# Modulation tiles in two buffers of their own, loaded from GpSimd's queue, and partly summed during the second V projection

## The chip, the cores and the metric

The kernel runs on one core of one Trainium2 chip. The metric is the device time of one execution in microseconds (us). A core has TensorE (PE, with its weight load PEld), VectorE (DVE), ScalarE (ACT), GpSimd (POOL) and SyncE (SP), each with an in-order instruction queue of its own. Loads are issued here from SyncE's queue, stores also from ScalarE's and GpSimd's.

## The reference

One layer of a backbone: x is (1, 512, 2048), the context (1, 256, 2048), all in float32.

```python
mx = silu(c) @ w_mod + b_mod                    # 2048 -> 6 x 2048: sh1, sc1, gt1, sh2, sc2, gt2
hc = modulate(rmsnorm(ctx, norm1_g), sh1c, sc1c)  # the same with c_ctx, for the context
hx = modulate(rmsnorm(x, norm1_g), sh1, sc1)
q, k, v, g, lf, lb, cb, cc, cx = split_proj(hx @ w_in)   # context: the same weights
o_x = gla_bidir(q, k, v, gates(lf), gates(lb), states of the context)  # 4 heads, chunks
mix = concat(rmsnorm(o_x) * gla_g * silu(g), cb * conv_grid(cc * cx, conv_w)) @ w_out
x = x + gt1 * mix
h2 = modulate(rmsnorm(x, norm2_g), sh2, sc2)
x = x + gt2 * (silu(h2 @ w_gate) * (h2 @ w_up)) @ w_down
return rmsnorm(x, final_g)
```

What matters here is the first line: the four later parts of the modulation, gt1, sh2, sc2 and gt2 (8192 numbers, each a product of silu(c) with 2048 weights), are not needed before the output projection.

## The kernel before

**Products.** Every large product runs on TensorE as three matmuls (`mm3`), of a high and a low part of both operands. A weight tile of 128 x 1024 is loaded into a buffer called `raw` (`load_raw`), cast on ScalarE to `whi` (line 102) and subtracted on VectorE to `wlo` (line 103); `whi` and `wlo` have three buffers each. A weight split in this text is line 103.

**Modulation tiles.** The 64 tiles of `wm2` hold the transposed weights of the four later parts: 128 outputs by 2048 inputs each. `mod_some(n, last)` adds n to what is owed and, for each whole tile owed, loads two halves of 128 x 1024 (512 KB each) into `raw` buffers. For each half VectorE multiplies by the broadcast silu(c) (`cbc`) and sums along the row (line 382, in the profile CUSTOM_DVE_ANT_0, followed by a short reading of the accumulator into `modacc`). These 128 are the sums of this text.

**Stages.** (1) scale and K projection; (2) first V projection (`wv[0]`), in which chunks of hx and hc are shifted as soon as they are used (`shift_chunk`, whose first step is an addition on GpSimd, and whose result also goes to the low-rank gate product, `lf_part`, `pl` in the profile); (3) second V projection (`wv[1]`, 16 steps of 18 matmuls, a weight tile for two steps), with the last four chunks shifted in its first four steps and then `shares`: sixteen more loads into `raw`, which TensorE multiplies directly (`pb`) to get the bias of K and V; (4) the weave: context states, gates, then four heads. In it `weave` takes turns between a stage of attention and a weight tile's worth of projection (`fill`), and calls `mod_some(MOD_STEP, 64)` after each, so that the modulation tiles are spread over the weave; (5) output projection and the feed-forward network.

**Order.** Up to the end of the weave a scheduler orders the instructions of every engine when the program is built: it takes what its own estimates say is ready first, with the order of the code as priority. So a load or a sum may stand well ahead of the place where the code has it. From the output projection on, SyncE's order is the code's. All raw loads, weights and modulation halves, go through SyncE's queue and take the next of four `raw` buffers; a load whose buffer is not free holds up all loads behind it.

Of the kernel before, what the change touches and what calls it, by code (L numbers as in the profile page):

```python
# [7 lines left out]
F32 = mybir.dt.float32  # L8
# [5 lines left out]
P = 128  # L14
# [39 lines left out]
def tile_hybrid_block(  # L54
# [6 lines left out]
    nc = tc.nc  # L61
# [3 lines left out]
    wpool = ctx.enter_context(tc.tile_pool(name="wpool", bufs=1))  # L65
# [14 lines left out]
    def bank(name="bank"):  # L80
        return pspool.tile([P, 512], F32, tag="g", name=name, bufs=5)

    def abank(name="abank"):
        return pspool.tile([P, 512], F32, tag="a", name=name, bufs=3)

    def banks6():
        return [abank("acc6") for _ in range(3)] + [bank("acc6") for _ in range(3)]

    def mm(o, l, r, start, stop):
        nc.tensor.matmul(o, l, r, start=start, stop=stop, skip_group_check=True)  # L90

    def mm3(o, l, r, start, stop):

        mm(o, l[1], r[0], start, False)
        mm(o, l[0], r[1], False, False)
        mm(o, l[0], r[0], False, stop)

    def sl(pair, *idx):
        return pair[0][idx], pair[1][idx]
# [12 lines left out]
        nc.scalar.activation(hi, src, AF.Identity, bias=shift)  # L112
        nc.vector.scalar_tensor_tensor(lo, src, shift, hi.bitcast(F32), op0=ALU.add, op1=ALU.subtract)

    def load_raw(src):
        n = src.shape[-1]
        r = wpool.tile([P, 1024], F32, tag="raw", name="raw", bufs=4)
        nc.sync.dma_start(r[:, :n], src)
        return r[:, :n]

    def load_w(src, k, eng=None):

        r = load_raw(src)
        n = r.shape[-1]
        hi = wpool.tile([P, 1024], F32R, tag="whi", name="whi", bufs=3)
        lo = wpool.tile([P, 1024], F32R, tag="wlo", name="wlo", bufs=3)
        split(hi[:, :n], lo[:, :n], r, eng)
        return (hi[:, :n].rearrange("p (k n) -> p k n", k=k),
                lo[:, :n].rearrange("p (k n) -> p k n", k=k))
# [179 lines left out]
    def shift_chunk(i):  # L309

        for n, h, rb, q in ((SEQ, hx[i], rbx, 0), (CTX, hc[i], rbc, 1)):
            t = hcpool.tile([P, n], F32, tag=f"sq{q}", name="ht", bufs=2)
            nc.gpsimd.tensor_tensor(t, h[0].bitcast(F32), h[1].bitcast(F32), op=ALU.add)
            nc.vector.tensor_tensor(t, t, rb, op=ALU.mult)
            sh = shs[:, i, q : q + 1]
            if q == 0:
                nc.vector.tensor_scalar(t, t, sh, None, op0=ALU.add)
                split(h[0], h[1], t)
                hraw[i] = t
            else:  # L320
                split_shifted(h[0], h[1], t, sh)

    def stat(i, tt):
        if tt < NX:
            return sl(hx[i], ALL, slice(tt * P, tt * P + P))
        return sl(hc[i], ALL, slice((tt - NX) * P, (tt - NX) * P + P))

    def lf_part(pl, i):
        j = 32 * (i % 4)
        mm(pl[j : j + 32, :], wl3[:, i, :], hraw[i], i < 4, i >= 12)  # L330

    def lf_finish(pl, a, n):

        t = hcpool.tile([P, SEQ], F32, tag="lfs", name="lfs", bufs=1)
        nc.scalar.copy(t[:, :n], pl[:, :n])
        ps = bank("ps")
        mm(ps[:32, :n], smt[:, S_QUAD : S_QUAD + 32], t[:, :n], True, True)
        nc.scalar.copy(lfT[:32, a : a + n], ps[:32, :n])
# [36 lines left out]
    def mod_some(n, last):  # L375

        owed[0] += n
        while owed[0] >= 1 and nmod[0] < last:
            j = nmod[0]
            for hf in range(2):  # L380
                w = load_raw(wm2[j][:, hf * 1024 : hf * 1024 + 1024])
                nc.vector.tensor_tensor_reduce(  # L382
                    out=w, in0=w, in1=cbc[:, hf * 1024 : hf * 1024 + 1024], scale=1.0, scalar=0.0,
                    op0=ALU.mult, op1=ALU.add, accum_out=modacc[:, j, hf : hf + 1])
            nmod[0] += 1
            owed[0] -= 1

    MOD_STEP = 0.85

    def mod_finish(a, b):  # L390
        nc.vector.tensor_tensor(modv[:, a:b], modacc[:, a:b, 0], modacc[:, a:b, 1], op=ALU.add)
        nc.vector.tensor_tensor(modv[:, a:b], modv[:, a:b], colt[:, C_BMOD + 32 + a : C_BMOD + 32 + b], op=ALU.add)


    def shares(i):
# [6 lines left out]
        if i % 8 == 0:  # L402
            sh_t["pb"] = bank("pb")
        pb = sh_t["pb"]
        w = load_raw((wk if i < 8 else wv[0])[i % 8]).rearrange("p (k n) -> p k n", k=2)
        for kk in range(2):
            k = 2 * (i % 8) + kk
            jj = 32 * (k % 4)
            mm(pb[jj : jj + 32, :], shs[:, k, :], w[:, kk, :], k < 4, k >= 12)
        if i % 8 == 7:  # L410
# [15 lines left out]
            else:  # L426
# [4 lines left out]
                for hh in range(2):  # L431
                    for t2 in range(2):
                        for u in range(2):
                            v = vx[hh][t2][:, u, :]
                            nc.vector.tensor_tensor(v, v, pbx[:, hh * DV : hh * DV + DV], op=ALU.add)
    sh_t = {}
    accv = banks6()
    for i in range(KD):
        if i % 2 == 0:
            wvp = load_w(wv[1, i // 2], 2)  # L440
        for tt in range(NX + NCT):
            mm3(accv[tt], stat(i, tt), sl(wvp, ALL, i % 2), i == 0, i == KD - 1)
        if i < 4:
            shift_chunk(KD - 4 + i)
        if i < 5:
            lf_part(pl, KD - 5 + i)
        elif i == 5:
            lf_finish(pl, 0, SEQ)
        else:
            for k in ((2 * i - 12, 2 * i - 11) if i < 12 else (i,)):  # L450
                shares(k)
# [83 lines left out]
    def weave(stages, fill):  # L535

        for _ in stages:
            next(fill, None)
            mod_some(MOD_STEP, 64)
        for _ in fill:  # L540
            mod_some(MOD_STEP, 64)

# [132 lines left out]
    for h in range(HEADS):  # L675
# [3 lines left out]
        if h + 2 < HEADS:  # L679
            fill.insert(0, do_q(h + 2))  # L680
        weave(do_gla(h), (None for g in fill for _ in g))
    mod_some(64, 64)
    mod_finish(0, 64)
    nc.vector.tensor_scalar(gsc2, modv[:, 32:48], 1.0, None, op0=ALU.add)
    nc.vector.tensor_tensor(gsc2, gsc2, colt[:, C_G2 : C_G2 + KD], op=ALU.mult)
# [256 lines left out]
    for p in range(NBD // 2):  # L942
# [20 lines left out]
        w = lambda b, u: wo[p, b, u]  # L963
# [280 lines left out]
```

## Time and profile before

| | us |
|---|---|
| median of 3 runs (2349.32 to 2352.01) | 2351.49 |
| the profiled execution | 2355.56 |
| its span, first to last instruction | 2353.8 |
| TensorE busy | 2270.1 |
| VectorE busy | 1671.7 |
| the 128 sums, busy | 156.4 |
| VectorE idle just ahead of the sums | 199.0 |
| first and last issue of a modulation load, from the span's start | 302.6, 831.2 |

The profile gives for a group of instructions how often it ran, the busy time, the mean of one, and the idle time of the engine just before it with what ended that idle time. `out<-in` are the program's names of tiles. In a timeline a row has start, duration, engine, line and, in brackets, the idle time before it. In a list of waits a row has who waited for whom, the sum in us, how often, and the longest.

### The profile page before, as it was taken

The numbers are of one execution on the slowest core, as the hardware profiler recorded it, in microseconds if no ns is written. First come the engines' busy times: TensorE is split into PE (matmuls) and PEld (weight loads), VectorE is DVE, ScalarE is ACT, GpSimd is POOL, SyncE is SP. The second block draws the span as 40 slices with busy tenths as digits, with TensorE's granted clock in tenths as the row PEclk, the third lists the DMA queues.
The fourth block names the chain that finished last, engine by engine and source line by source line (L and its number), as shares of the span: only waits on it lengthen the run. The fifth ranks groups of instructions, "written<-read, shape, count | busy, mean of one in ns | idle before, by whom it ended". The sixth has DMA issues, their size and how long they took to land.

```text
span 2353.8 us, 27801 instructions
## 1 busy us (share of the span) xinstructions
PE 2270.1 (96%) x10328; PEld 1807.0 (77%) x10328; DVE 1671.7 (71%) x2066; ACT 1002.5 (43%) x1349; POOL 136.1 (6%) x186
## 2 busy tenths in 40 slices
PE   8999999999989899999999999999999999999996
PEld 4765667787777778787888888888888878888875
DVE  3566164665555757779888788878887877787888
ACT  3433055233232324465544554455445544443343
POOL 2423000000000000000000000000000000000001
PEclk9999999999999999999999999999999999999998
DMA  9773365666656654544434643464345585756634
GB/s 329 225 258 121 134 223 171 202 195 193 196 188 189 205 183 147 179 155 126 160 117 152 205 144 120 149 206 144 125 143 206 191 316 178 274 176 198 243 128 137
DMA packets 161619, 431.43 MB, mean 183 GB/s; under 512 B 17867, under 2 KB 38635, under 8 KB 161356
## 3 DMA queue, kind: packets, MB, share of 16 engines
q1 hardware_dynamic: 141612, 380.87, 49.2%
q0 software_dynamic: 8720, 28.58, 3.2%
q10 hardware_dynamic: 11152, 20.21, 2.3%
q8 instruction: 81, 1.33, 0.2%
q14 instruction: 54, 0.44, 0.1%
HBM read 380.82 MB, written 48.78 MB: 183 GB/s over the span
## 4 chain that ended last, share of the span: by engine, by line
PE 50%; DVE 5%; DMA 2%; issue 1%; ACT 1%; SPq 0%; POOL 0%; DVEq 0%; POOLq 0%; ACTq 0%
PE acc L90 49%; DVE wlo L103 2%; DMA raw<-wd 1%; PE pt L990 1%; DMA raw<-wu 1%; PE pt L90 1%; DVE y L1102 0%; DVE y L1122 0%; ACT whi L102 0%; DVE ch L818 0%; DVE y L1114 0%; DMA ch<-wd 0%; DVE y L1113 0%; DVE ch L799 0%; DVE hbig L959 0%
## 5 line engine op out<-in xcount | busy, mean ns | idle before, releaser
L102 ACT CAST whi<-ch 128x1024 fp32r<-128x1024 f32 x350 | 368.7, 1054 | 433.4 <-PE acc L90 361.2
L103 DVE TENSOR_TENSOR wlo<-ch,whi 128x1024 fp32r<-128x1024 f32 x350 | 425.9, 1221 | 139.2 <-ACT whi L102 138.1
L102 ACT CAST whi<-raw 128x1024 fp32r<-128x1024 f32 x252 | 264.4, 1051 | 438.8 <-PE acc L90 250.5
L103 DVE TENSOR_TENSOR wlo<-raw,whi 128x1024 fp32r<-128x1024 f32 x252 | 312.0, 1239 | 168.4 <-ACT whi L102 167.8
L382 DVE CUSTOM_DVE_ANT_0 raw<-raw,cbc 128x1024 f32<-128x1024 f32 x128 | 156.4, 1224 | 199.0 <-DMA raw<-wm 196.1
L90 PE MATMUL acc<-hhl,whi 128*128 128x512 f32 x640 | 201.2, 395 | 0.0
L90 PE MATMUL acc<-hhi,wlo 128*128 128x512 f32 x320 | 135.5, 425 | 17.8 <-DVE wlo L103 17.1
L90 PEld LDWEIGHTS acc<-hhl,whi 128*128 128x128 f32 x640 | 122.2, 191 | 28.2 <-issue 2.5
L90 PE MATMUL acc<-hhl,wlo 128*128 128x512 f32 x320 | 128.4, 401 | 0.0
L90 PE MATMUL acc<-hlo,whi 128*128 128x512 f32 x320 | 127.5, 399 | 0.2 <-DVE hlo L108 0.2
L90 PE MATMUL acc<-hhi,whi 128*128 128x512 f32 x320 | 127.6, 399 | 0.0
L90 PE MATMUL acc<-whi,a6l 128*128 128x512 f32 x312 | 122.7, 394 | 4.0 <-DVE big L838 2.6
L90 PE MATMUL acc<-wlo,a0h 128*128 128x512 f32 x312 | 123.3, 395 | 2.1 <-DVE wlo L103 2.1
L90 PE MATMUL acc<-wlo,a6h 128*128 128x512 f32 x312 | 122.7, 393 | 0.9 <-DVE wlo L103 0.9
L90 PE MATMUL acc<-whi,a6h 128*128 128x512 f32 x312 | 122.6, 393 | 0.0
L90 PE MATMUL acc<-wlo,a5h 128*128 128x512 f32 x312 | 121.7, 390 | 0.9 <-DVE wlo L103 0.9
L90 PE MATMUL acc<-whi,a0h 128*128 128x512 f32 x312 | 122.3, 392 | 0.0
L90 PE MATMUL acc<-whi,a0l 128*128 128x512 f32 x312 | 121.8, 391 | 0.0
L90 PE MATMUL acc<-whi,a5l 128*128 128x512 f32 x312 | 121.5, 389 | 0.0
L90 PE MATMUL acc<-whi,a5h 128*128 128x512 f32 x312 | 121.5, 389 | 0.0
L90 PE MATMUL acc<-whi,a2l 128*128 128x512 f32 x280 | 109.7, 394 | 4.8 <-ACT whi L102 4.8
L90 PE MATMUL acc<-wlo,a1h 128*128 128x512 f32 x280 | 109.2, 390 | 1.5 <-DVE wlo L103 1.5
(301 smaller groups left out, 4761.6 us busy)
## 6 DMA issues: line engine op xcount, KB each, us to landing
raw<-wm SPq DMA_DIRECT2D x128, 512.0 KB, 4.7
raw<-wu SPq DMA_DIRECT2D x92, 512.0 KB, 4.4
ch<-wu SPq DMA_DIRECT2D x88, 512.0 KB, 3.8
raw<-wc SPq DMA_DIRECT2D x48, 512.0 KB, 4.0
raw<-wd SPq DMA_DIRECT2D x47, 512.0 KB, 6.6
ch<-wd SPq DMA_DIRECT2D x44, 512.0 KB, 5.9
opd<-oh ACTq DMA_DIRECT2D x77, 256.0 KB, 3.0
opd<-ol POOLq DMA_DIRECT2D x77, 256.0 KB, 3.5
```

The lines of the kernel that those rows point to most:

```text
L90: nc.tensor.matmul(o, l, r, start=start, stop=stop, skip_group_check=True)
L102: nc.scalar.copy(hi, src)
L103: (eng or nc.vector).tensor_tensor(lo, src, hi, op=ALU.subtract)
L382: nc.vector.tensor_tensor_reduce(out=w, in0=w, in1=cbc[:, hf * 1024 : hf * 1024 + 1024], scale=1.0, scalar=0.0, op0=ALU.mult, op1=ALU.add, ...
L990: nc.tensor.transpose(pt[:, (2 * i + t) * P : (2 * i + t) * P + P], acts[j][2 * hf + t][:, q * P : q * P + P], ident)
```

## The change

`load_raw` gets a flag `mod`. A modulation half goes into a buffer of the tag `raw2` (two buffers) and its load is issued from GpSimd. While `mod_room` is set, from the second V projection to the end of the weave, all other raw loads use the tag `raw` (two buffers); outside of it they alternate between the two tags. `mod_some(1, 64)` is called in each of the 16 steps of the second V projection, and MOD_STEP falls from 0.85 to 0.65.

```diff
+    nraw, mod_room = [0], [False]
+
+    def load_raw(src, mod=False):
+
         n = src.shape[-1]
-        r = wpool.tile([P, 1024], F32, tag="raw", name="raw", bufs=4)
-        nc.sync.dma_start(r[:, :n], src)
+        nraw[0] += 1
+        second = mod if mod or mod_room[0] else nraw[0] % 2
+        r = wpool.tile([P, 1024], F32, tag="raw2" if second else "raw", name="raw", bufs=2)
+        (nc.gpsimd if mod else nc.sync).dma_start(r[:, :n], src)
         return r[:, :n]
...
-                w = load_raw(wm2[j][:, hf * 1024 : hf * 1024 + 1024])
+                w = load_raw(wm2[j][:, hf * 1024 : hf * 1024 + 1024], True)
...
-    MOD_STEP = 0.85
+    MOD_STEP = 0.65
...
     sh_t = {}
+    mod_room[0] = True
     accv = banks6()
     for i in range(KD):
...
             mm3(accv[tt], stat(i, tt), sl(wvp, ALL, i % 2), i == 0, i == KD - 1)
+        mod_some(1, 64)
...
     mod_some(64, 64)
+    mod_room[0] = False
     mod_finish(0, 64)
```

The scheduler moves the sums further than the code does. On VectorE, before, the late part of the second V projection reads as follows (the accumulator readings behind each sum are left out, here and below; `acc6_1874` is an accumulator of that projection, copied at its end, `raw_` with `cbc` is a sum):

```order
L103 TENSOR_TENSOR wlo_2277<-raw_2274,whi_2276 128x1024
L103 TENSOR_TENSOR wlo_2331<-raw_2328,whi_2330 128x1024
L103 TENSOR_TENSOR wlo_2436<-raw_2433,whi_2435 128x1024
L103 TENSOR_TENSOR wlo_2479<-raw_2476,whi_2478 128x1024
L382 ISA raw_2506,modacc_73<-raw_2506,cbc_76 128x1024
L382 ISA raw_2509,modacc_73<-raw_2509,cbc_76 128x1024
L459 COPY big_2410<-acc6_1874 128x512
```

There the last two weight splits of the projection and two of the next stand ahead of the first two sums of the program. Now, between the same last two weight splits:

```order
L103 TENSOR_TENSOR wlo_2349<-raw_2346,whi_2348 128x1024
L387 ISA raw_2974,modacc_73<-raw_2974,cbc_76 128x1024
L387 ISA raw_2977,modacc_73<-raw_2977,cbc_76 128x1024
L387 ISA raw_3043,modacc_73<-raw_3043,cbc_76 128x1024
L387 ISA raw_3046,modacc_73<-raw_3046,cbc_76 128x1024
L387 ISA raw_3079,modacc_73<-raw_3079,cbc_76 128x1024
L103 TENSOR_TENSOR wlo_2415<-raw_2412,whi_2414 128x1024
L387 ISA raw_3082,modacc_73<-raw_3082,cbc_76 128x1024
```

Five sums stand between two splits, each behind its own load. Counted over the whole order, 17 sums stand ahead of the first V projection's end, 53 ahead of the second's, and all 128 ahead of the middle of head 1; before, these were 0, 2 and some 60.

On GpSimd, before, at the last of the shifted chunks (`ht` is the addition that begins a chunk's shift; `hbig` with MEMSET clears a mask buffer for the heads):

```order
L313 TENSOR_TENSOR ht_1930<-hhl_890 128x512
L313 TENSOR_TENSOR ht_1966<-hhi_966,hlo_967 128x512
L313 TENSOR_TENSOR ht_1996<-hhl_1007 128x512
L552 MEMSET hbig_2659 128x512
L552 MEMSET hbig_2661 128x512
L961 DMA xnd_5897<-xn_6080 128x512
L961 DMA xnd_5897<-xn_6082 128x512
```

And now, at the same place:

```order
L318 TENSOR_TENSOR ht_1984<-hhi_966,hlo_967 128x512
L123 DMA raw_2294<-wm2 128x1024
L318 TENSOR_TENSOR ht_2020<-hhl_1007 128x512
L123 DMA raw_2328<-wm2 128x1024
L123 DMA raw_2331<-wm2 128x1024
L123 DMA raw_2370<-wm2 128x1024
L123 DMA raw_2373<-wm2 128x1024
L123 DMA raw_2400<-wm2 128x1024
L123 DMA raw_2403<-wm2 128x1024
L123 DMA raw_2436<-wm2 128x1024
L123 DMA raw_2439<-wm2 128x1024
L559 MEMSET hbig_2743 128x512
```

The modulation loads stand between the chunks' additions, and each of them waits for the sum two halves before it, and with it what is behind it on GpSimd.

More of the change, by code (lines that the diff above doesn't have):

```diff
@@ L113, in split_shifted @@
         nc.vector.scalar_tensor_tensor(lo, src, shift, hi.bitcast(F32), op0=ALU.add, op1=ALU.subtract)
-    def load_raw(src):
+    nraw, mod_room = [0], [False]
+    def load_raw(src, mod=False):
         n = src.shape[-1]
-        r = wpool.tile([P, 1024], F32, tag="raw", name="raw", bufs=4)
-        nc.sync.dma_start(r[:, :n], src)
+        nraw[0] += 1
+        second = mod if mod or mod_room[0] else nraw[0] % 2
+        r = wpool.tile([P, 1024], F32, tag="raw2" if second else "raw", name="raw", bufs=2)
+        (nc.gpsimd if mod else nc.sync).dma_start(r[:, :n], src)
         return r[:, :n]
```

## The prediction

> **What bounds the kernel now.** I read the page first (busy shares, then the groups), then who waited for whom in three stretches, then the timeline of VectorE and GpSimd where the change puts its work.
>
> ```profile
> PE 2270.1 (96%) x10328; PEld 1807.0 (77%) x10328; DVE 1671.7 (71%) x2066; ACT 1002.5 (43%) x1349; POOL 136.1 (6%) x186
> L382 DVE CUSTOM_DVE_ANT_0 raw<-raw,cbc 128x1024 f32<-128x1024 f32 x128 | 156.4, 1224 | 199.0 <-DMA raw<-wm 196.1
> ```
>
> TensorE is busy nearly throughout, so time can only come from its gaps. The second row is what the change touches: 128 half-tile sums on VectorE, 1.22 us each, before which VectorE idled 196 us waiting for their own loads. A table by stretch shows where TensorE has gaps: the second V projection (213 to 311 us), the context, the gates and head 0 (311 to 550), heads 1 to 3 (550 to 850).
>
> ```profile
> core 0: us, PE busy (x) PEld busy (x) DVE busy (x) ACT busy (x) POOL busy (x), PEclk, DMA share, GB/s
> 213.00:311.00 98.00, 97.56 (x455) 63.53 (x453) 27.40 (x40) 17.65 (x30) 8.26 (x8) 1.00 0.39 129
> 311.00:550.00 239.00, 229.31 (x995) 178.68 (x993) 144.70 (x242) 103.36 (x141) 0.00 (x0) 0.98 0.62 197
> 550.00:850.00 300.00, 276.15 (x1236) 225.63 (x1236) 184.62 (x326) 89.28 (x159) 0.00 (x0) 0.97 0.60 190
> ```
>
> The V projection has no gap worth naming, its VectorE is idle for 71 of 98 us, and its granted clock is 1.00. The middle stretch has 9.7 us of gaps, heads 1 to 3 have 23.85, and both run below full clock. Who ends TensorE's gaps in heads 1 to 3, and what VectorE itself waited for there:
>
> ```profile
> PE acc L90 <- DVE wlo L103: 8.6, 7, 2.5
> PE pd L90 <- DVE hbig L606: 5.0, 2, 4.1
> PE po L90 <- ACT sm L620: 4.3, 5, 1.5
> PE psc L90 <- DVE ke L589: 4.2, 1, 4.2
> PE psc L90 <- ACT a0h L102: 1.1, 1, 1.1
> DVE raw L382 <- DMA raw<-wm: 114.2, 48, 5.7
> ```
>
> Three of the five are VectorE being late (17.8 us), and the one thing VectorE waited for at length is the modulation tile at the head of its queue, behind which weight splits and head work stand.
>
> **The change, part by part.** No instruction is added or removed: 128 loads of 512 KB move from SyncE's queue to GpSimd's; the four raw buffers become two for weights and two for modulation halves; and the sums move forward. By the order of the built program, VectorE has 17 sums ahead of the copies that end the first V projection (0 before), 53 ahead of those that end the second (2 before), and all 128 ahead of the weight split that ran at 550.02 us (60 ahead of it and 68 behind it before), so heads 1 to 3 have nearly none left. I price the four stretches apart.
>
> **The pace of a sum.** With two buffers, each holds a half for one round trip: the sum, the handover to GpSimd, the load, the wake of VectorE. These rows price it:
>
> ```profile
> 306.34 1.23 DVE L382 CUSTOM_DVE_ANT_0 raw<-raw,cbc 128x1024 f32<-128x1024 f32 x1 [1.24 <-DMA raw<-wm]
> 1145.04 0.68 DVE L103 TENSOR_TENSOR ol<-pt,oh 128x512 fp32r<-128x512 f32 x1
> 1146.12 0.54 POOL L1004 DMA_DIRECT2D opd<-ol  x1 [2.76 <-DVE ol L103]
> DMA to landing us min/median/max: 3.5/4.7/7.2
> opd<-oh ACTq DMA_DIRECT2D x77, 256.0 KB, 3.0
> opd<-ol POOLq DMA_DIRECT2D x77, 256.0 KB, 3.5
> ```
>
> The sum takes 1.23; from the end of a VectorE operation to the GpSimd load that waited for it pass 1146.12 - 1145.72 = 0.4. The landing row is that of the 128 modulation loads. GpSimd's issue lands 0.5 later than ScalarE's of the same size (last two rows). No row shows a 512 KB load from GpSimd. Its lower bound is the fastest landing seen, 3.5; its upper bound is the median and the 0.5, 5.2. Before, up to four raw loads stood in one queue; now at most two halves do, beside one or two weights, so I take the middle, 4.35, and 0.1 for the wake. A round trip is 1.23 + 0.4 + 4.35 + 0.1 = 6.1 us, and two buffers give a sum each 3.05 us (2.6 to 3.45 at the bounds).
>
> By the Trainium skill (DMA: Bandwidth & Descriptors, the section on the anatomy of one DMA on the GpSimd path) such a load takes about 2.0 us and its bytes over 436 GB/s, which for 512 KB makes 3.2 us, a pace of 2.5 us and, by the sum below, the 2321.5 us of the second rival; the trace has no 512 KB load from GpSimd to set against it, and the quickest one from SyncE took 3.5.
>
> **First V projection: +1 us.** The 17 sums (21 us) lie in VectorE's idle time there. GpSimd's additions, with which the shift of a chunk starts, now stand behind loads that wait for a sum. The tightest chunk shows what that may cost (its shifted value, then TensorE's use of it):
>
> ```profile
> 171.32 0.48 DVE L317 TENSOR_SCALAR ht<-ht,silsh 128x512 f32<-128x512 f32 x1
> 177.79 1.04 PE L90 MATMUL pl<-ht,big 128*32 128x512 f32 x2
> ```
>
> It is ready 6 us early, which one sum and part of a load's wait fill without harm; I leave 1 us (0 to 5).
>
> **Second V projection: +18 us.** Here the cover is gone, because VectorE works in order and the splits that feed TensorE now stand behind sums:
>
> ```profile
> 234.82 0.69 DVE L103 TENSOR_TENSOR hhl<-ht,hhl 128x512 fp32r<-128x512 f32 x1 [0.74 <-ACT hhl L102]
> 258.34 1.23 DVE L103 TENSOR_TENSOR wlo<-raw,whi 128x1024 fp32r<-128x1024 f32 x1 [22.83 <-ACT whi L102]
> 294.33 1.23 DVE L103 TENSOR_TENSOR wlo<-raw,whi 128x1024 fp32r<-128x1024 f32 x1 [7.44 <-ACT whi L102]
> 311.16 1.28 DVE L459 COPY big<-acc 128x512 f32<-128x512 f32 x2
> 550.02 1.23 DVE L103 TENSOR_TENSOR wlo<-raw,whi 128x1024 fp32r<-128x1024 f32 x1 [1.18 <-ACT whi L102]
> ```
>
> The first row is the last shifted chunk. Between it and the next weight split now stand 11 sums, then 6, 5 and 5 between the later splits and 4 up to the copy of 311.16: 31 in all. The chunk ends at 235.5; the five sums put among the chunks before it delay it by 3 us, to 238.5. Two halves are already loaded (2 x 1.2), 29 come at the pace: 238.5 + 2.4 + 29 x 3.05 = 329.4, against 311.2, so +18. With pace 2.6 it is 316.3 (+5), with 3.45 it is 341 (+30). A floor comes from the other half of the edit: weights and the sixteen bias loads (pb) now share two buffers, and each is reloaded only when TensorE or the split has let go of it. Four weight tiles stand behind such loads, and four are waited for already:
>
> ```profile
> raw<-wv SPq DMA_DIRECT2D x12, 512.0 KB, 4.2
> ACT whi L102 <- DMA raw<-wv: 39.7, 4, 11.8
> ```
>
> With a landing of 4.2 us that is mostly under TensorE's work I estimate 2 us more for each of the four, so the stretch loses at least 8.
>
> **Context, gates and head 0: -3 us.** From the copy at 311.16 to the split at 550.02 are 239 us, with 58 sums before and 75 now. At the pace these are 229 us. VectorE's other work there (144.7 busy less 58 x 1.23, 73 us) mostly fits into the 3.6 us that a pair of sums leaves idle; where it stands in clusters it doesn't (the row of copies and additions after 311.16, the products of head 0), and I put 10 us for these: 239, so 0. VectorE was ahead of need there:
>
> ```profile
> 558.08 0.58 PE L90 MATMUL acc<-hhi,wlo 128*128 128x512 f32 x1
> ```
>
> TensorE took that split up 6.8 us after its end; I let half of this stock go, so -3. It cannot gain more than its gaps (9.7) and the clock (2% of 239, 4.8): -14. With pace 3.45 it is 259 + 10 - 239 - 3 = +27.
>
> **Heads 1 to 3: -25 us.** With no sum left, VectorE loses 114 us of waiting and its lateness. Gaps ended by VectorE go (17.8); the chain of ScalarE's scaled states (5.4 together) stays, since its links are not the sums. The clock row, 0.97 of 300 us, is 9 us of slower matmuls behind such gaps, of which I take 7. Bounds: -13 (only the weight splits, 8.6, and half of the clock) and -33 (23.85 + 9). The work behind the last sum (mod_finish) has 300 us more time; nothing waits for it earlier.
>
> After the weave the loads alternate between the two pairs, which is four buffers in turn as before: 0.
>
> **Sum:** +1 + 18 - 3 - 25 = -9 us. The profiled execution (span 2353.8, 2355.56 with what lies around it) would come to 2346.5; the median of the runs is 4.1 lower, 2351.5, so I forecast 2342.5. Each 0.1 us of pace moves the sum by 2.9 + 7.5 = 10.4 us, so this forecast is a balance of two large terms.
>
> **Rivals.** (1) Slower: the round trip of the modulation buffers becomes the bound of everything up to head 1. It decides from a pace of 3.14 us, a landing of 4.5. For it: the median landing now is 4.7 from a quicker queue. Against it: the halves' own queue is nearly empty. At pace 3.3 (landing 4.85) the sum is +17: 2368.5. (2) Well faster: the landing is near its minimum, 3.5 to 3.9, TensorE bounds the middle again, and the sum is +1 + 8 - 14 - 25 = -30: 2321.5 (with the largest head gain, 2313.5). (3) No change: the heads keep their gaps because ScalarE's chain, not VectorE, sets them (-15 in place of -25): +1, 2352.5. (4) The change does not do what it says: in the built order it is not 16 tiles by the second projection's end but 26; had it been 16, the V term would be at its floor of 8; the built order is what the sums above count.
>
> **Chances.** Forecast (-20 to -5 us) 0.33; rival 1 0.30; rival 2 0.20; rival 3 0.17. A change within 0.2% (4.7 us) is what a measurement here cannot tell from none. So faster 0.53, same 0.17, slower 0.30. The range runs from 2317 (most of rival 2) to 2372 (rival 1 up to pace 3.33); alone, the likeliest case has 2331 to 2347.
>
> **What would show it.** Right: VectorE's wait for the modulation load remains, now before 560 us and not after; the second V projection ends near 330; TensorE's gaps in heads 1 to 3 shrink to some 6 us and the clock there rises to 0.99 or more. GpSimd's loads land in about 4.3 us. Wrong: landings of 4.7 or more (then the split that ran at 550 comes later than 565 and the time rises), of under 3.9 (then the projection ends before 322), or gaps in heads 1 to 3 that stay with ScalarE's chain at their head.

## The result, and the profile after

The changed kernel took 2386.35 us (median; 2383.88 to 2392.41) against 2350.88 of the kernel before on the same chip: 1.0149 times as long, with a 95% interval of 1.0132 to 1.0166. It is slower by 35 us, where 9 us less had been forecast. The profiled execution took 2392.41 us, with a span of 2390.6.

The page after, TensorE and the group of the sums (count, busy time and mean of one, idle time just before them):

```profile
PE 2286.1 (96%) x10328; PEld 1814.8 (76%) x10328; DVE 1678.0 (70%) x2066; ACT 1004.1 (42%) x1349; POOL 207.3 (9%) x314
L387 DVE CUSTOM_DVE_ANT_0 raw<-raw,cbc 128x1024 f32<-128x1024 f32 x128 | 158.4, 1239 | 169.0 <-DMA raw<-wm 168.8
```

VectorE's wait for the modulation loads fell from 196 to 169 us, and the kernel still became slower. So what counts is where these waits stand. I cut both traces at the same work: the first matmul of the second V projection (214 us before, 231 after), of the weave's first weight tile (311, 366), of the tile whose split ran at 550 (558, 639) and of the last tiles of the weave (895, 935). The stretches before, in the columns of the prediction's table:

```profile
118.00:214.00 96.00, 93.99 (x444) 57.40 (x445) 58.05 (x89) 29.74 (x47) 24.77 (x22) 1.00 0.65 222
214.00:311.00 97.00, 97.00 (x452) 63.38 (x449) 27.05 (x39) 16.93 (x28) 8.26 (x8) 1.00 0.39 128
311.00:558.00 247.00, 236.20 (x1024) 184.09 (x1023) 150.14 (x250) 105.95 (x145) 0.00 (x0) 0.98 0.62 197
558.00:895.00 337.00, 312.37 (x1391) 255.73 (x1391) 196.09 (x343) 96.82 (x171) 1.23 (x2) 0.96 0.59 189
```

The same work after:

```profile
118.00:231.00 113.00, 99.34 (x446) 60.28 (x445) 76.03 (x119) 27.42 (x42) 35.85 (x40) 0.92 0.75 257
231.00:366.00 135.00, 113.81 (x452) 67.97 (x450) 71.40 (x114) 18.71 (x35) 29.49 (x45) 0.90 0.70 230
366.00:639.00 273.00, 249.11 (x1023) 192.62 (x1024) 169.35 (x282) 107.05 (x145) 38.78 (x73) 0.93 0.64 210
639.00:935.00 296.00, 296.00 (x1387) 248.37 (x1386) 120.60 (x205) 96.97 (x170) 0.84 (x2) 1.00 0.30 96
```

First V projection +17 us, second +38, context, gates and head 0 +26, the heads behind them -41: +40 in all, of which some 3 us come back behind the weave. The heads do what was hoped, and more: TensorE is busy in all 296 us, at full clock. The three stretches that took in the sums pay 81 us for it. Each pays twice: in the second V projection TensorE has 21.2 us of gaps (0 before), and its matmuls, at a clock of 0.90 in place of 1.00, take 16.8 us longer (113.81 - 97.00). In the heads both come back: 24.6 us of gaps and 16.4 of slower matmuls.

The sums of the first three stretches, one row each, and the landing of their loads:

```profile
L387 DVE CUSTOM_DVE_ANT_0 raw<-raw,cbc 128x1024 f32<-128x1024 f32 x16 | 20.4, 1274 | 25.5 <-DMA raw<-wm 25.4
L387 DVE CUSTOM_DVE_ANT_0 raw<-raw,cbc 128x1024 f32<-128x1024 f32 x37 | 46.4, 1253 | 59.7 <-DMA raw<-wm 59.7
L387 DVE CUSTOM_DVE_ANT_0 raw<-raw,cbc 128x1024 f32<-128x1024 f32 x75 | 91.7, 1224 | 83.8 <-DMA raw<-wm 83.7
raw<-wm POOLq DMA_DIRECT2D x128, 512.0 KB, 4.6
```

The second V projection holds 37 sums in 135 us, one in 3.65; the next stretch 75 in 273, one in 3.64. That the two buffers set this pace the trace shows: from the start of a sum to that of the sum two later, which takes the same buffer, pass 7.2 us on average in the first of these stretches and 6.9 in the second. Of these, 0.4 to 0.5 go to the issue of the next load, 4.9 and 4.7 to its landing, 0.6 until the sum starts and 1.2 to the sum. This is the first rival's picture.

In the first V projection the loads fall into the bursts in which SyncE loads `wsh`. One such chain, from the timelines of GpSimd, VectorE, ScalarE and TensorE:

```profile
189.62 0.57 POOL L123 DMA_DIRECT2D raw<-wm  x1 [1.50 <-DVE modacc L387]
198.00 1.23 DVE L387 CUSTOM_DVE_ANT_0 raw<-raw,cbc 128x1024 f32<-128x1024 f32 x1 [3.86 <-DMA raw<-wm]
199.15 0.48 DVE L322 TENSOR_SCALAR ht<-ht,silsh 128x512 f32<-128x512 f32 x1
199.72 0.62 ACT L102 CAST hhl<-ht 128x512 fp32r<-128x512 f32 x1 [7.22 <-DVE ht L322]
201.19 0.58 ACT L223 COPY tm<-pm 128x512 f32<-128x512 f32 x1
201.82 1.86 PE L90 MATMUL pc<-smt,tm 128*128 128x2 f32 x8 [6.62 <-ACT tm L223]
```

The load took 8.4 us to land. The sum at the head of VectorE's queue held the shift of a chunk, this held ScalarE's cast, behind which stood the copy of a shift row's product, and TensorE stood still for 6.62 us. An idle VectorE did not help: what it was to do next stood behind the sum.

That is one half of the stretch's 13.7 us of gaps. The other is TensorE waiting for `wsh` itself, whose loads in this stretch landed in 5.6 us at the median before and in 6.7 now. TensorE's wait for them, before and after:

```profile
PE pm L90 <- DMA big<-wsh: 2.0, 3, 0.8
PE pm L90 <- DMA big<-wsh: 7.0, 3, 3.4
```

### The profile page after: what moved, and what is told of

Its sections match the earlier page's. It is cut to its first block, busy times and chain, and to the rows that moved or that the text cites. A ratio compares the mean times of both kernels' runs of the same rounds, so it can differ in the third digit from the quotient of the medians.

```text
span 2390.6 us, 27833 instructions
## 1 busy us (share of the span) xinstructions
PE 2286.1 (96%) x10328; PEld 1814.8 (76%) x10328; DVE 1678.0 (70%) x2066; ACT 1004.1 (42%) x1349; POOL 207.3 (9%) x314
## 4 chain that ended last, share of the span: by engine, by line
issue 52%; PE 36%; DVE 4%; POOL 4%; DMA 3%; ACT 1%; POOLq 0%; SPq 0%; DVEq 0%; ACTq 0%
PE acc L90 32%; DMA raw<-wm 2%; POOL raw L123 2%; DVE wlo L103 2%; POOL opd L1012 1%; PE pm L90 1%; PE pt L90 1%; PE po L90 1%; DVE raw L387 0%; ACT whi L102 0%; POOL out L1131 0%; PE pd L90 0%; DMA raw<-wk 0%; PE pl L90 0%; PE pc L90 0%
## 5 line engine op out<-in xcount | busy, mean ns | idle before, releaser
L102 ACT CAST whi<-ch 128x1024 fp32r<-128x1024 f32 x350 | 368.9, 1054 | 430.9 <-PE acc L90 361.1
L102 ACT CAST whi<-raw 128x1024 fp32r<-128x1024 f32 x252 | 264.7, 1051 | 481.9 <-PE acc L90 292.3
L1012 POOL DMA_DIRECT2D opd<-ol x77 | 41.8, 543 | 880.4 <-DVE ol L103 880.4
```

What stands on the lines that cost most here:

```text
L102: nc.scalar.copy(hi, src)
L1012: nc.gpsimd.dma_start(opd[j][i, 1].rearrange("p k t -> p (k t)"), lo.bitcast(F32))
```

## Experiments: what the parts cost

All ratios are to the kernel before, run on the same chip. The line of the sums, 382 before and 387 after, is another by a few in some of these kernels.

**The queue alone** (`e1`). Edit against the kernel before:

```diff
-    def load_raw(src):
+    def load_raw(src, mod=False):
...
-        nc.sync.dma_start(r[:, :n], src)
+        (nc.gpsimd if mod else nc.sync).dma_start(r[:, :n], src)
...
-                w = load_raw(wm2[j][:, hf * 1024 : hf * 1024 + 1024])
+                w = load_raw(wm2[j][:, hf * 1024 : hf * 1024 + 1024], True)
```

> The kernel before, with the modulation loads issued from GpSimd and nothing else changed: four shared buffers, the sums where they stood before (in the built order none ahead of the first V projection's end, 0 ahead of the second's last splits, 60 ahead of the split that ran at 550 us, the same counts as in the kernel before). Theory 1 (the loss comes from the order: sums that stand ahead of the weight splits and wait there for a round trip through two buffers): V projections within 1 us of before, all of it within 10 us of before (2341 to 2361). Rival (GpSimd's queue itself is the cause, its landings are longer or disturb SyncE's loads): slower by 15 us or more, 2366 upwards, with the loss in the weave.

2376.65 us, 1.0106 (1.0083 to 1.0130), 28.6 us slower, all of it in the weave: my theory that only the order counts fell here. VectorE's wait for these loads in the weave, before and here:

```profile
DVE raw L382 <- DMA raw<-wm: 194.8, 91, 5.7
DVE raw L382 <- DMA raw<-wm: 224.3, 97, 5.4
```

It waits 29.5 us more, about as much as the kernel lost. The landing is not the reason (median 4.6 us here, 4.7 before). The handover is what differs: on SyncE a load that waited for a sum is issued 0.03 us after the end of its reading (658.78, rows further down), on GpSimd 0.4 us after VectorE lets the buffer go:

```profile
488.21 1.22 DVE L103 TENSOR_TENSOR wlo<-raw,whi 128x1024 fp32r<-128x1024 f32 x1
489.83 0.53 POOL L118 DMA_DIRECT2D raw<-wm  x1 [7.12 <-DVE wlo L103]
```

Nearly all of the 128 loads show the same two figures, 0.41 here and 0.03 before. One handover for each of the 64 tiles, at 0.4 us, would make 26 us. This is an estimate, and this run alone does not show that the handover is the whole cause. What it shows is that in the kernel before the waits in the weave were not spare: lengthening them lengthened the program.

**The buffers alone** (`e2`): the changed kernel with the loads on SyncE's queue, without the calls, MOD_STEP 0.85. The line of the queue:

```diff
-        (nc.gpsimd if mod else nc.sync).dma_start(r[:, :n], src)
+        nc.sync.dma_start(r[:, :n], src)
```

> The changed kernel with the modulation loads back on SyncE's queue, and without the calls in the second V projection: buffers of their own alone. In the built order 4 sums stand ahead of the first V projection's end, 38 ahead of the second's (changed kernel 10 and 53 by the same count, before 0 and 0). Theory 1 (the order): the loss of the V projections shrinks with the sums ahead, to some 4 us in the first and 25 in the second (changed kernel 16.5 and 39), total 2360 to 2380. Rival (GpSimd's queue is the cause): V projections within 5 us of before and a total below 2350.

2344.60 us, 0.9982 (0.9966 to 0.9999). Both expectations hold in part: the total is the rival's, but the second V projection still lost 23 us, as the order would have it, and the heads gave back 39. Queue and buffers thus are 29 and -3 us alone and 35 together.

**The calls** (`e12`): the changed kernel without `mod_some(1, 64)` in the second V projection and with the old MOD_STEP.

```diff
-    MOD_STEP = 0.65
+    MOD_STEP = 0.85
...
-        mod_some(1, 64)
```

> The changed kernel without the calls in the second V projection and with MOD_STEP 0.85 as before. The counts of sums at every place are those of the changed kernel. Theory (own buffers move the sums forward, and the calls and the step change nothing): within 5 us of the changed kernel, 2381 to 2391. Rival (the calls matter): below 2375.

2389.03 us, 1.0158 (1.0129 to 1.0187): no change. The calls in the second V projection, the last part of the change's title, do nothing. With own buffers the scheduler moves the sums forward by itself, as far as it believes the loads to be there.

**No sum before a given point** (`e3`, `e4`). The silu(c) that every sum reads is made to depend on the last copy of the first V projection (`vc[NCT - 1][0]`), or of the second (`[1]`, the lines moved behind it, without the calls and with the old MOD_STEP); the edit of `e3`:

```diff
-    nc.scalar.activation(cbc, cbc, AF.Silu)
+    late = cpool.tile([P, 1], F32, name="late")
+    nc.vector.tensor_scalar(late, vc[NCT - 1][0][:, 0:1], 0.0, 1.0, op0=ALU.mult, op1=ALU.add)
+    nc.scalar.activation(cbc, cbc, AF.Silu, scale=late)
```

> The changed kernel, with the silu(c) that the sums need made to depend on the last copy of the first V projection, so that no sum can stand ahead of its end (built order: 0 there, 37 ahead of the second projection's end, 115 ahead of the split that ran at 550). Theory 1: the 16.5 us of the first projection come back whole, the second loses by its sums, about 37/53 of 39, 27 us; the rest as in the changed kernel (mid +25, heads -40): total near 2363 (2355 to 2372). Rival (two buffers for the weights, not the sums, slow the second projection): it still loses 35 us or more, total 2370 or above.

> The same with the dependence on the last copy of the second V projection: no sum ahead of it (built order 0 there, 77 ahead of the split that ran at 550, all 128 ahead of head 2). Theory 1: both V projections within 3 us of before; the middle stretch slower by some 20 us, the heads faster by 30: total near 2342 (2333 to 2356). Rival (two buffers for the weights and the bias loads): the second projection still loses 15 us or more, although not one sum stands in it, and the total is above 2356.

2376.64 us (1.0105, 1.0077 to 1.0133) and 2376.99 us (1.0112, 1.0078 to 1.0147). With no sum in the first projection its loss is gone whole (0.0 us against before), so the sums there, with their loads, cost the 16.5 us. But then the second projection lost 43.9 us, not 27. The two in `e3`:

```profile
118.00:214.00 96.00, 93.94 (x443) 57.36 (x445) 56.81 (x89) 26.45 (x45) 25.80 (x24) 1.00 0.65 222
214.00:355.00 141.00, 112.23 (x455) 67.08 (x451) 69.71 (x114) 20.47 (x31) 27.77 (x45) 0.90 0.66 217
```

And with no sum in either, the second still lost 18: the rival's case.

**Two buffers for the weights** (`e5`): `e4`, with `mod_room` set only behind the second V projection.

```diff
-    mod_room[0] = True
     accv = banks6()
...
+    mod_room[0] = True
     lf_finish(sh_t["pl"], SEQ, CTX)
```

> The kernel of the run with no sum ahead of the second V projection's end, but now the weights and the sixteen bias loads of that projection alternate between both pairs of raw buffers (the weights are confined to one pair only after it). That run lost 18 us in the projection without a sum in it. Theory (two raw buffers for weights and bias loads cost it): the projection is back within 3 us of the kernel before, the total 15 us below that run, near 2362 (2355 to 2368). Rival (the loss came from something else, such as the loads already waiting on GpSimd): it still loses 12 us or more, total 2372 or above.

2359.00 us, 1.0035 (1.0019 to 1.0051), 18 us below `e4`. The second projection of `e4` and of `e5`:

```profile
214.00:330.00 116.00, 106.89 (x459) 66.05 (x459) 26.58 (x41) 16.54 (x29) 8.25 (x8) 0.94 0.31 101
214.00:311.00 97.00, 97.00 (x453) 63.76 (x452) 26.21 (x39) 17.11 (x29) 9.49 (x10) 1.00 0.35 121
```

So confining eight weight tiles and sixteen bias loads to two buffers costs some 18 us by itself. The versions on GpSimd's queue now make a ladder: 2359 with own buffers and the sums behind the V projections, 2377 with two buffers for the second projection's weights, 2377 with the sums in it as well (what they cost there, the heads give back), and 2386 to 2389 with sums in the first projection.

## Experiments: a head start for the loads

In the kernel before, the weave reads like this on VectorE and SyncE (timelines; the accumulator's readings and small copies are left out):

```profile
657.52 1.22 DVE L382 CUSTOM_DVE_ANT_0 raw<-raw,cbc 128x1024 f32<-128x1024 f32 x1
658.78 1.65 SPq L118 DMA_DIRECT2D raw<-wm  x2
664.85 1.23 DVE L382 CUSTOM_DVE_ANT_0 raw<-raw,cbc 128x1024 f32<-128x1024 f32 x1 [2.86 <-DMA raw<-wm]
666.12 1.23 DVE L382 CUSTOM_DVE_ANT_0 raw<-raw,cbc 128x1024 f32<-128x1024 f32 x1
667.27 1.22 DVE L103 TENSOR_TENSOR wlo<-raw,whi 128x1024 fp32r<-128x1024 f32 x1
```

The sums free the buffers, the next two loads go out, and the next sum that VectorE meets is theirs; the weight split stands behind it. The scheduler puts a sum where it expects its load, and the load comes later than that. So I tied each tile's two sums to the latest weight cast, by a write of two numbers of that cast into the place of their result:

```diff
+    cast = [None]
...
         split(hi[:, :n], lo[:, :n], r, eng)
+        cast[0] = hi
...
             j = nmod[0]
+            nc.scalar.copy(modacc[:, j, :], cast[0][:, 0:2].bitcast(F32))
             for hf in range(2):
```

It went into `e5` (GpSimd's queue, own buffers) in place of the dependence of silu(c), into the same with SyncE's queue, and into the kernel before (shared buffers, SyncE).

> As the run before, and each modulation tile's two sums are tied to the latest weight cast (ScalarE writes two numbers of that cast into the place of their result first), so that VectorE's order spreads them: 14 to 16 in eight weight tiles, 56 ahead of the split that ran at 550, in place of 17 to 22 and 78. Own buffers and GpSimd's queue stay. Theory 1 (what costs is sums standing closer together than a buffer's round trip of 6.5 us, 3.4 a sum): VectorE waits less than 40 us for these loads (169 in the changed kernel), no stretch is slower than before by over 5 us, total 2318 to 2343. Rival (GpSimd's queue costs by itself, as with shared buffers, where it lost 28 us): total 2360 or above.

> The same with the modulation loads on SyncE's queue. Theory 1: the same within 5 us (2318 to 2345), since the loads are issued a weight tile ahead of their use on either queue. Rival A (the handover of 0.4 us and the queue matter): faster than GpSimd's by 8 us or more. Rival B (a modulation load whose buffer is taken holds up the weights behind it on SyncE): slower than GpSimd's by 8 us or more.

> The kernel before (four shared buffers, SyncE's queue) with nothing but the tie of each tile's sums to the latest weight cast. Counts of sums by place within 4 of the kernel before. Theory (the even spacing alone is worth something): 2330 to 2345. Rival (what the kernel before loses is loads that stand behind other raw loads for a shared buffer, so own buffers are needed): within 5 us of before, 2343 to 2353.

2298.22 us (0.9779, 0.9745 to 0.9813), 2294.60 us (0.9776, 0.9731 to 0.9820) and 2293.70 us (0.9761, 0.9727 to 0.9795). All three beat both kernels; I had expected the first two 20 to 50 us slower, and that the shared buffers would be as good I had not expected at all: both cases of `e8` missed. The sums in the three pages:

```profile
L389 DVE CUSTOM_DVE_ANT_0 raw<-raw,cbc 128x1024 f32<-128x1024 f32 x128 | 155.3, 1222 | 105.6 <-DMA raw<-wm 100.9 <-ACT po L649 1.7 <-ACT on L648 1.4
L389 DVE CUSTOM_DVE_ANT_0 raw<-raw,cbc 128x1024 f32<-128x1024 f32 x128 | 155.1, 1222 | 58.8 <-DMA raw<-wm 55.1 <-ACT po L649 1.6 <-ACT modacc L386 1.2
L386 DVE CUSTOM_DVE_ANT_0 raw<-raw,cbc 128x1024 f32<-128x1024 f32 x128 | 152.9, 1220 | 11.9 <-DMA raw<-wm 8.7 <-issue 1.9 <-ACT modacc L383 1.2
```

In the last one VectorE hardly waits any more. The place in its trace that answers to the one above, and its weave (context to head 0, then the heads):

```profile
646.63 1.47 SPq L120 DMA_DIRECT2D raw<-wm  x2
658.51 1.23 DVE L103 TENSOR_TENSOR wlo<-raw,whi 128x1024 fp32r<-128x1024 f32 x1 [5.87 <-ACT whi L102]
659.65 1.22 DVE L386 CUSTOM_DVE_ANT_0 raw<-raw,cbc 128x1024 f32<-128x1024 f32 x1
659.76 1.47 SPq L120 DMA_DIRECT2D raw<-wm  x2
...
315.00:544.00 229.00, 229.00 (x1028) 182.30 (x1027) 148.49 (x246) 111.83 (x175) 0.00 (x0) 1.00 0.63 210
544.00:840.00 296.00, 296.00 (x1388) 248.40 (x1387) 198.55 (x345) 101.63 (x203) 0.65 (x1) 1.00 0.66 218
```

The split goes first, the sum behind it, and its load is long there (loads that were under way at 646.63 had landed by 653.5). TensorE is busy without a gap at full clock with the same 128 sums, in shared buffers and at a higher rate than before (first to last sum 475 us in place of 530). So what this pair differs by is not room, nor the number of sums per microsecond, but when a split gets its turn. The traces show it for each pair with and without the tie. From the end of a weight's cast on ScalarE to the start of its split on VectorE, the average of the weave's 80 splits is 5.8 us before and 0.3 here, 3.8 in `e5` and 1.8 in `e6`, 6.2 in `e1` and 0.4 with the tie (`e11` below).

How long VectorE waits in all is another matter. In `e6` I had expected under 40 us of waits for the loads; there are 100.9, and the kernel is only 4.5 us behind `e8`. From the end of the second projection on, `e5` and `e6`:

```profile
311.00:580.00 269.00, 241.30 (x1022) 186.23 (x1021) 173.12 (x287) 109.03 (x147) 42.31 (x80) 0.97 0.65 217
311.00:560.00 249.00, 249.00 (x1115) 198.91 (x1115) 162.53 (x273) 121.02 (x197) 34.77 (x66) 1.00 0.65 213
```

VectorE still waits 40.6 us for the loads in the second row, and TensorE has no gap: these waits hold no split for long. Most of the gain, then, is there although the loads still come late. The 4.5 us between `e6` and `e8` no run divides among loads in time, queue and buffers.

The first V projection of `e8` took 4.6 us more than before, with no sum in it. There TensorE waited 3.8 us for `wsh` in place of 2.0, and its clock was 0.97 (118 to 219 us) in place of 1.00; why, I did not follow up.

**Is it the head start, or the tie as such?** (`e9`): `e6` with the sums too close for two buffers.

```diff
-    MOD_STEP = 0.85
+    MOD_STEP = 1.3
```

> The paced kernel with GpSimd's queue and own buffers (MOD_STEP 0.85, 2298.2 us), now with MOD_STEP 1.3: 20 to 24 sums in eight weight tiles in place of 14, 85 ahead of the split that ran at 550 in place of 56, the tie kept. Eight weight tiles take TensorE some 58 us when it isn't held up, so that is a sum every 2.4 to 2.9 us, under the 3.4 us that a sum through two buffers took. Theory 1 (spacing against the round trip decides): slow again, near the unpaced kernel with the same buffers (2359), 2350 to 2385, with VectorE waiting over 130 us for the loads. Rival (the tie helps in another way, say by the priority it gives the weight splits): under 2320.

2372.45 us, 1.0089 (1.0065 to 1.0113): slow again, with the tie in place, and the splits start 4.2 us after their casts. So the tie helps only as long as the sums are not closer together than the buffers' round trip allows. VectorE's wait:

```profile
DVE raw L389 <- DMA raw<-wm: 135.8, 90, 3.5
```

**The change with the tie** (`e10`), **and the queue with the tie** (`e11`: the kernel before with GpSimd's queue, as `e1`).

> The changed kernel as it is (own buffers, GpSimd's queue, calls in the second V projection, MOD_STEP 0.65) with the tie alone added: now 0 sums ahead of the first V projection's end, 32 ahead of the second's, 76 ahead of the split that ran at 550, 122 ahead of the middle of head 2. Theory 1: the first projection as before; the second loses the 18 us that two raw buffers cost it, and up to 11 more, because 32 sums in 98 us are one in 3.06; the weave gains some 50: total 2312 to 2330. Rival (the work in the second projection is harmful by itself): 2340 or more.

> The kernel before with GpSimd's queue for the modulation loads (which alone cost 28 us) and the tie. Theory 1 (the 0.4 us handover counts only where VectorE waits for the load): 2290 to 2302. Rival (GpSimd's queue costs by itself): 2315 or more.

2322.43 us, 0.9874 (0.9850 to 0.9897), and 2296.09 us, 0.9764 (0.9743 to 0.9785), both as expected. `e10` now does what the title says (32 sums in the second V projection); it still loses there, and gains in the weave (second projection, to head 0, heads):

```profile
220.00:340.00 120.00, 104.73 (x451) 63.64 (x450) 57.77 (x91) 18.95 (x44) 23.27 (x34) 0.94 0.62 205
340.00:572.00 232.00, 229.37 (x1025) 182.69 (x1023) 133.94 (x219) 111.35 (x169) 24.34 (x46) 0.99 0.56 181
572.00:868.00 296.00, 296.00 (x1387) 248.39 (x1386) 179.05 (x309) 100.61 (x193) 26.05 (x50) 1.00 0.56 186
```

Its second projection takes 120 us in place of 97, of which the two buffers are 18. In `e11` the queue that cost 28 us costs 2, which is within the spread of the runs. So a handover of 0.4 us costs next to nothing once the splits go first, though VectorE still waits 41 us for the loads there.

## Why the prediction was wrong

What came nearest was rival 1: the round trip through two buffers bounds the second V projection, the middle and head 0. I had given it 0.30, and its price, 2368.5, was too low as well: it had neither the loss of the first V projection nor the full price of two buffers for the weights. By steps, measured to the tenth at the cuts above:

- **The pace of a sum.** Sum, handover and wake were right: 1.22 to 1.25, 0.4 and 0.13 us. The landing, which I put at 4.35 between 3.5 and 5.2, had a median of 4.6, and reached 8.6 in the bursts. With it a round trip is 6.4 us, 3.2 a sum. The average landing, 4.9 us in the second V projection, and some 0.4 us until VectorE was free of other work, of which I spread 10 us over one stretch, bring it to 3.6. By my own sum 3.6 in place of 3.05 makes the second V projection +34 and the middle +38 (which counts the 10 us twice); 39.3 and 24.7 came. The Trainium skill (DMA: Bandwidth & Descriptors, the section on the anatomy of one DMA on the GpSimd path) has a fit by which such a load takes 3.2 us, an estimate. The trace has 4.6 at the median and none under 3.7, and that case, 2321.5, did not come.
- **First V projection, +1; measured +16.5.** The failed step is "lie in VectorE's idle time". I looked for harm on GpSimd's additions and found 6 us of room, but the harm came in two other ways, each about half of the gaps. By VectorE: a landing of 6.7 to 8.6 us beside the `wsh` bursts, with the chain shown above behind it. And by the `wsh` tiles, which came later themselves. That SyncE loads some 60 of them in this stretch the profile of before shows (its DMA share is 0.65 there); I didn't ask whom the loads would meet.
- **Second V projection, +18; measured +39.3.** The count of sums was near (31 forecast between the last shifted chunk and the copy, 37 in all between the cuts), the pace wasn't. And the floor for the two raw buffers, 8, was 18 by `e4` and `e5`: 2 us for each of four tiles was a guess, beside a row, "ACT whi L102 <- DMA raw<-wv: 39.7", that had shown ScalarE waiting for these loads already.
- **Context, gates, head 0, -3; measured +24.7.** Again the pace: 75 sums in 273 us. That VectorE was "ahead of need", from one split 6.8 us early, did not hold for the stretch: before, TensorE had waited there twice for a split, 4.1 us in all.
- **Heads 1 to 3, -25; measured -40.1.** Here I was too careful, beyond my bound of -33. ScalarE's chain went with the rest: its scaled states had waited 65 us for VectorE (from 558 to 895 us), and wait 6 now. And the slower matmuls gave back 16.4 us; I had taken 7, reading only the clock column.
- **Rival 4** was right in its half: the change's calls do nothing (`e12`). **Rival 3** was wrong, and with rival 2 it had 0.37.

The deeper miss is in the first part. I read VectorE's idle time as cover that could be used ("idle for 71 of 98 us"), and its 196 us of waiting as a cost only where a gap of TensorE named VectorE. The total is neither a cover nor a price. In `e1` 29.5 us more of it cost 28.6, here 27 us less came with a loss of 35, and `e6` wins 51 with 101 us of it left. What counts is whether a split stands behind the wait. That half, that a sum is put where the scheduler believes its load to be, and every split behind it pays when it isn't, stood in my text as a reason for +18 and not as a way to price the whole weave.

## What to carry to other kernels

On an in-order engine the idle time ahead of a filler operation is no free room: the work behind it waits too, so put the filler behind the urgent operation, with its load a full step ahead, before adding buffers or a queue. The engine's total of waits doesn't price this; how late the urgent operation starts does. When buffers limit a stream, its pace is the round trip with everything that the engine does in between, and it has to be compared with the pace at which the order asks for it. And a buffer taken from one stream for another has a price of its own, to be measured alone.

## What the runs showed of the hardware

- The granted clock falls with gaps of under 3 us. After the change the longest gap that ended in the second V projection was this one:

```profile
290.38 0.80 PE L90 MATMUL acc<-wlo,hhi 128*128 128x512 f32 x1 [2.74 <-DVE wlo L103]
```

  The stretch's gaps sum to 21.2 us, its clock is 0.90 and its matmuls took 16.8 us more; in the heads before, 24.6 us of gaps went with 16.4 us, in the stretch between, 13.1 us more gap with 12.9. So here a microsecond of gap went with 1.7 to 2 us of lost time, its own included. The 0.90 is a mean of two values: cut finely, the clock there is 1.00 or 0.50. It is 0.50 from 289.55 to 296.3 us, for one, and in the 3.4 us ahead of that TensorE was busy for 1.05. The Trainium skill (TensorE: Matmul & The Clock Gate, part 1) has the clock halved after an idle window of some 3.4 us; no gap of that stretch was so long, and the clock fell all the same.
- A load of 512 KB landed as late from GpSimd's queue as from SyncE's (medians 4.6 and 4.7 us). The 0.5 that the prediction added for GpSimd came from transfers of 256 KB out of the core, and from a comparison with ScalarE (3.5 and 3.0). But from a buffer's release to the issue pass 0.4 us on GpSimd and 0.03 on SyncE.
- Beside 16 loads of 256 KB in a burst, a load of 512 KB took up to 8.6 us to land, and the burst's own loads up to 10.3 (7.6 before, without it).
